# Fifteen tiles of a vector-by-matrix product: from GpSimd and ScalarE to TensorE

## The chip, the cores and the metric

The kernel runs on one core of a Trainium2 chip. A core has five engines that run side by side, each with its own queue of instructions in program order: TensorE (PE in the profile, with its weight loads shown apart as PEld), VectorE (DVE), ScalarE (ACT), GpSimd (POOL) and SyncE (SP), which issues most of the transfers from the chip's memory. The metric is the device time of one execution in microseconds (us), and the median of the runs counts.

## The reference

The program is one encoder block on 256 tokens of width 1024, in float32. What the change touches is the first line of it, the adaLN modulation: one vector of 1024 numbers goes through silu and a 1024 x 6144 matrix, and the six parts of the result shift, scale and gate everything else.

```
c_act = silu(c)
ada = c_act @ w_ada + b_ada
shift1, scale1, gate1, shift2, scale2, gate2 = split(ada, 6)

h = rms_norm(x, norm1_g) * (1 + scale1) + shift1
proj = h @ w_in
mixed = concat(rms_norm(windowed_gqa(...)), rms_norm(neighbourhood_attention(...)))
x = x + gate1 * (mixed @ w_out)
h2 = rms_norm(x, norm2_g) * (1 + scale2) + shift2
x = x + gate2 * peer(h2, w_query, sub_keys, u_experts, v_experts)
return rms_norm(x, final_g)
```

`peer` picks experts for each token out of 16,384 and costs by far the most: two matrices of 16,384 x 1024 are read whole.

## The kernel before

The execution falls into two halves. In the first, up to about 224 us, a planner orders everything from the modulation to the queries of `peer`; in the second, lines 1366 to 1583 write out by hand the passes over the two expert matrices, 128 tiles of 128 x 1024 each (lines 1507 and 1557), with rows gathered beside them by GpSimd (line 1421).

In the first half each piece of work is a job: it names one engine (or several to choose from) with a cost in us, the jobs that it needs, and the buffers or PSUM banks that it takes and frees. `run_plan` (line 295) tries 300 random orders with those costs, keeps the one in which TensorE ends first, and emits the instructions in that order. On each engine they then stand in a fixed order. So a changed cost or engine moves instructions all over the first half, and `ROUNDS`, `SEED` and the costs set the order.

All weight tiles are 128 partitions x 1024 float32 (512 KB), loaded by SyncE in the order of `STREAM` (lines 62 and 687) into nine early buffers and then eight buffers used in turn; a load waits until its buffer is free. What becomes of a tile:

- `w_in`, `w_out` and `w_query` tiles are split into a high and a low half so that a matmul of three fast products gives float32 precision: ScalarE writes the high half (line 626), VectorE or GpSimd subtracts it for the low half (line 630, later 398). The matmuls are lines 806 (the first twelve tiles, all eight chunks of the input in turn) and 442 (the rest), 24 instructions of 256 columns a tile.
- `w_ada` tiles (48, one for each 128 outputs) are laid out with the output on the partitions. `ca` holds silu(c) copied to all partitions. On VectorE one instruction multiplies the tile by `ca` and sums along the row (line 606). Fifteen tiles, those of `ON_POOL`, are done in two steps instead: GpSimd multiplies (line 598), ScalarE sums (line 601). All fifteen belong to gate1, scale2 and shift2. Eight more, of gate2, are done in the second half on VectorE.

Between the input projections and the output projection stand eight pairs of heads: scores (lines 925, 927), bias and maximum on VectorE (945), exponent on ScalarE (949), weights (982), transposes (999, 1002), values (1021, 1025), and the norms (750). Gate1 is first used at line 1077, shift2 and scale2 at 1092 to 1107. The first half ends with the sums for the second norm (line 750 again), two queries in float32 (1113), one query in split halves (1144), and from line 1358 the scores of `peer`.

Of the kernel before, what the change touches and what calls it, by code (L numbers as in the profile page):

```python
# [12 lines left out]
AF = mybir.ActivationFunctionType  # L13
# [3 lines left out]
P = 128  # L17
D = 1024
NC8 = 8
# [16 lines left out]
NCST = _o  # L36

SHIFT1, SCALE1, GATE1, SHIFT2, SCALE2, GATE2 = range(6)
ON_POOL = {(GATE1, 0), (GATE1, 2), (GATE1, 3), (GATE1, 5), (GATE1, 7), (SCALE2, 0), (SCALE2, 1), (SCALE2, 2), (SCALE2, 4), (SCALE2, 5), (SCALE2, 6), (SHIFT2, 1), (SHIFT2, 2), (SHIFT2, 3), (SHIFT2, 4)}
RAW = 4  # L40
SETTLE = 6.0
SETS = (64, 32)
# [17 lines left out]
LO_POOL = 1  # L60
# [5 lines left out]
def kernel(ctx: ExitStack, tc: tile.TileContext, xT, crow, vecs, cst, w_ada, w_in, w_out,  # L66
# [11 lines left out]
    V, S, PE, G = nc.vector, nc.scalar, nc.tensor, nc.gpsimd  # L78
# [7 lines left out]
    ada = keep.tile([P, 6, 8], F32, name="ada")  # L86
# [3 lines left out]
    cs = keep.tile([P, 8], F32, name="cs")  # L90
# [54 lines left out]
    def add(alts, *deps, take=(), free=(), lag=0.0, after=None, rows=P):  # L145
        return Job(alts, deps, take, free, lag, after, rows)
# [174 lines left out]
    MM = 0.1095  # L321
# [16 lines left out]
    tiles = {}  # L338
# [125 lines left out]
    ca = carve(D)  # L464
# [52 lines left out]
    def silu(y, x):  # L517
        S.activation(y, x, AF.Exp, scale=-1.0)
        V.tensor_scalar(y, y, 1.0, None, op0=ALU.add)
        V.reciprocal(y, y)  # L520
        V.tensor_mul(y, y, x)

    silu(c8t[:8], c8[:8])
    for w, part in ((0, SCALE1), (1, SCALE2)):
        a0 = VEC["b_ada"][0] + part * 8
        V.scalar_tensor_tensor(gb[:, w, :], vec[:, a0:a0 + 8], 1.0, v_("g2" if w else "g1"),
                               op0=ALU.add, op1=ALU.mult)
# [19 lines left out]
    cas = []  # L547
    for w in range(2):
        key = ("ca", w)
# [6 lines left out]
        m = add([("pe", 0.86, spread_c)], take=[("bank", key)], rows=8)  # L556
# [33 lines left out]
    column = {}  # L590

    def load_ada(part, c):
        key = ("ada", part, c)
        m = load(w_ada[part, c], key)
        col = ada[:, part, c:c + 1]
        if (part, c) in ON_POOL:
            def mul():
                G.tensor_mul(tiles[key], tiles[key], ca)

            def total():  # L600
                S.activation(tiles[key], tiles[key], AF.Copy, accum_out=col)

            m = add([("pool", 2.3, mul)], m, *cas)
            column[part, c] = add([("act", 1.04, total)], m, free=[key])
        else:
            column[part, c] = add([("dve", 1.15, lambda: V.scalar_tensor_tensor(
                tiles[key], tiles[key], 1.0, ca, op0=ALU.mult, op1=ALU.mult, accum_out=col))], m, *cas, free=[key])

    halved = {}
# [4 lines left out]
    def load_w(kind, i):  # L614
        key = ("w", kind, i)
        m = load(SRC[kind][i], key)
        hkey = ("h", kind, i)
        held_key[kind, i] = hkey
        if (kind, i) in WHOLE or kind == "q" and i < NQ:
            halved[kind, i] = whole[kind, i] = m  # L620
            held_key[kind, i] = key
            return

        def high():
            halves[kind, i] = new_halves(got(hkey))
            S.activation(halves[kind, i][0], tiles[key].rearrange("p (c n) -> p c n", n=P), AF.Copy)

        def low(e):
            hi, lo = halves[kind, i]
            e.tensor_sub(lo, tiles[key].rearrange("p (c n) -> p c n", n=P), hi.bitcast(F32))  # L630

        a = add([("act", 0.95, high)], m, take=[("split", hkey)])
        halved[kind, i] = add([("dve", 1.14, lambda: low(V))] + [("pool", 2.3, lambda: low(G))] * LO_POOL, a, free=[key])


    lscr = dram.tile([8, 512], F32, name="lscr")
# [1 line left out]
    def line_mm():  # L638
        PE.matmul(take_bank("line").rearrange("p a b -> p (a b)")[:8, :], t5s[:32], onehs[:32], start=True, stop=True)

    m = add([("pe", 0.86, line_mm)], take=[("bank", "line")], rows=32)
    m = add([("dve", 0.65, lambda: V.tensor_add(line[:8], tiles["line"].rearrange("p a b -> p (a b)")[:8, :], maska[:8]))],
            m, free=["line"])
# [122 lines left out]
    m = None  # L766
    for i in range(4):
        a = add([op("act", c_act(512), S.activation, sq[:, 2 * i:2 * i + 2, :], xs[:, 2 * i:2 * i + 2, :],
                    AF.Square)], xin[i])
        if i:  # L770
            a = add([op("dve", c_dve(512), V.tensor_add, sq[:, 0:2, :], sq[:, 0:2, :], sq[:, 2 * i:2 * i + 2, :])], a, m)
        m = a
# [865 lines left out]
def _layout(np, i):  # L1638
    def cols(v):
        return v.reshape(-1, P).T  # L1640

    def tiles(w):
        return w.reshape(8, P, -1, P).transpose(2, 1, 0, 3).reshape(-1, P, D)

    pa = np.array([j + 4 * s for j in range(4) for s in range(2)])
    fa = (pa[:, None] * 64 + np.arange(64)[None]).reshape(-1)
    vec = np.concatenate([
        cols(i["c"][0]),
        i["b_ada"][0].reshape(6, 8, P).transpose(2, 0, 1).reshape(P, 48),
        cols(i["norm1_g"][0]), cols(i["norm2_g"][0]), cols(i["final_g"]),  # L1650
        cols(i["out_norm_a"][0][fa]), cols(i["out_norm_b"][0]),
        np.broadcast_to(i["sink_a"][0][pa][None], (P, 8)),
    ], axis=1)
    w_in = i["w_in"][0]
    order = [np.arange(512, 640)] + [fa[j * P:(j + 1) * P] for j in range(4)] + [np.arange(640, 768)]
    for j in range(4):
        for s in range(3):
            order.append(768 + 512 * s + j * P + np.arange(P))
    w_in = tiles(w_in[:, np.concatenate(order)]).reshape(18, P, 8, P)
    first = []  # L1660
    for cp in range(4 if KT == 12 else 0):
        for c in (2 * cp, 2 * cp + 1):
            first.append(w_in[0:8, :, c].transpose(1, 0, 2))
        first.append(w_in[8:12, :, 2 * cp:2 * cp + 2].transpose(1, 2, 0, 3).reshape(P, 8, P))
    for c in range(8 if KT == 16 else 0):
        for k in range(2):
            first.append(w_in[8 * k:8 * k + 8, :, c].transpose(1, 0, 2))
    w_in = np.concatenate([np.stack(first), w_in[KT:]]).reshape(18, P, D)
    w_out = i["w_out"][0]
    w_out = np.concatenate([w_out[:512][fa], w_out[512:]], axis=0)  # L1670
    w_out = w_out.reshape(2, 4, P, 4, 2, P).transpose(0, 3, 2, 4, 1, 5).reshape(8, P, D)
    rpb = np.stack([i["rpb_b"][0].reshape(4, 2, 465)[:, :, 108 + 31 * r:264 + 31 * r] for r in range(4)])
    rpb = rpb.transpose(2, 0, 1, 3).reshape(-1)
    return {
        "xT": i["x"][0].T.reshape(8, P, T).transpose(1, 0, 2),
        "crow": i["c"].reshape(8, P),
        "vecs": vec,
        "cst": _constants(np),
        "w_ada": i["w_ada"][0].T.reshape(6, 8, P, D),
        "w_in": w_in,  # L1680
        "w_out": w_out,
        "w_query": tiles(i["w_query"][0]),
        "t5": i["t5_table"][:, pa],
        "rpb": rpb,
        "skT": i["sub_keys"][0].reshape(16, P, P).transpose(2, 0, 1),
        "uT": i["u_experts"][0].reshape(NE, P, 8, P).transpose(0, 3, 2, 1).reshape(NE, P, D),
        "uE": i["u_experts"][0],
        "vE": i["v_experts"][0],
    }
# [20 lines left out]
```

## Time and profile before

| | |
|---|---|
| median of 3 runs | 850.65 us (848.18 to 851.6) |
| the profiled execution's own time | 850.8 us |
| its span in the profile | 849.0 us |
| TensorE busy | 775.2 us, 91% |
| VectorE busy | 593.1 us, 70% |
| ScalarE busy | 268.0 us, 32% |
| GpSimd busy | 330.6 us, 39% |
| mean granted TensorE clock | 0.976 of full speed |
| bytes moved | 289.27 MB, 341 GB/s over the span |

The span is the time from the first to the last instruction that the profile shows; what lies around it, 1.8 us here, is not shown. "Busy" counts an engine's instructions whatever they wait for inside; an instruction that takes longer than its like is busy all that time. Shares over the span hide that the two halves have different limits, so the rows below are by stretch.

### The profile page before, as it was taken

How to read it: one execution, taken by the hardware profiler on the slowest of the kernel's cores; microseconds unless marked ns; L12 is line 12 of the kernel's file. 1: busy time of each engine (PE TensorE's matmuls, PEld its weight loads, DVE VectorE, ACT ScalarE, POOL GpSimd, SP SyncE). 2: the span in 40 equal slices, each digit the busy share in tenths (PEclk: the TensorE clock that was granted, in tenths of full speed). 3: DMA queues.
4: the chain of work that ended last, by engine and by line, in shares of the span. 5: the costliest groups of instructions: out<-in, count | busy, mean ns of one | idle time of the engine just before them, and what ended most of it. 6: DMA issues, size and time to landing. Idle time of an engine off the chain costs nothing.

```text
span 849.0 us, 15375 instructions
## 1 busy us (share of the span) xinstructions
PE 775.2 (91%) x5846; PEld 753.9 (89%) x5846; DVE 593.1 (70%) x1308; ACT 268.0 (32%) x741; POOL 330.6 (39%) x271
## 2 busy tenths in 40 slices
PE   3998786789799999999999999999999989899894
PEld 1997575689799999999999999999999988899893
DVE  6999999887677999569998775644435444453534
ACT  4456675456231112179876521000000000000003
POOL 2545686456314436412233233533333333332300
PEclk9999998999999999999999999999999999999997
DMA  8995666095768999999999999999999999999951
GB/s 328 408 328 206 223 227 234 0 348 202 259 229 297 392 413 395 416 413 361 359 378 374 401 371 416 415 412 416 415 416 415 414 415 416 415 413 418 414 205 50
DMA packets 81212, 289.27 MB, mean 341 GB/s; under 512 B 9281, under 2 KB 10825, under 8 KB 81010
## 3 DMA queue, kind: packets, MB, share of 16 engines
q1 hardware_dynamic: 36352, 125.60, 38.5%
q0 software_dynamic: 27776, 100.79, 30.2%
q10 hardware_dynamic: 17010, 61.89, 18.4%
q8 instruction: 46, 0.75, 0.4%
q14 instruction: 28, 0.23, 0.1%
HBM read 287.18 MB, written 1.07 MB: 340 GB/s over the span
## 4 chain that ended last, share of the span: by engine, by line
PE 34%; DMA 28%; issue 5%; DVE 3%; POOL 3%; ACT 0%; DVEq 0%; ACTq 0%; POOLq 0%
PE b L1507 27%; DMA row<-in_vE,big 24%; PE b L1557 4%; DMA raw<-in_vE,big 3%; PE b L1474 2%; DVE accg L1443 1%; POOL row L1421 1%; DMA row<-in_uT 1%; POOL raw L1421 1%; DMA row<-in_vE 1%; PE b L1342 1%; PE b L1562 0%; POOL big L1421 0%; DVE big L1443 0%; POOL lo L398 0%
## 5 line engine op out<-in xcount | busy, mean ns | idle before, releaser
L1507 PE MATMUL b<-big 128*128 128x160 f32 x928 | 134.3, 302 | 4.0 <-ACT big L1489 4.0
L1557 PE MATMUL b<-big 128*128 128x160 f32 x944 | 131.0, 299 | 5.0 <-DMA big<-in_vE 4.2
L1557 PEld LDWEIGHTS b<-big 128*128 128x128 f32 x944 | 129.0, 190 | 5.7 <-DMA big<-in_vE 4.7
L1557 PE MATMUL b<-big,row 128*128 128x160 f32 x864 | 125.5, 305 | 7.4 <-DMA row<-in_vE 7.4
L1507 PEld LDWEIGHTS b<-big 128*128 128x128 f32 x928 | 128.4, 191 | 4.2 <-ACT big L1489 4.2
L1557 PEld LDWEIGHTS b<-big,row 128*128 128x128 f32 x864 | 121.8, 194 | 8.1 <-DMA row<-in_vE 4.3
L1507 PE MATMUL b<-big,row 128*128 128x160 f32 x752 | 106.6, 300 | 0.0
L1507 PEld LDWEIGHTS b<-big,row 128*128 128x128 f32 x752 | 103.0, 190 | 0.0
L540 ACT ACTIVATE big<-xs 128x256 f32<-128x256 f32 (+1 forms) x20 | 9.1, 457 | 283.8 <-DVE xs L540 273.8
L1421 POOL DMA_INDIRECT row<-in_vE,big x48 | 49.9, 1039 | 88.0 <-DVE accg L1443 58.5
L1443 DVE SCALAR_TENSOR_TENSOR accg<-row,big,accg 128x1024 f32<-128x1024 f32 x32 | 41.2, 1286 | 51.2 <-DMA row<-in_vE,big 48.4
L442 PE MATMUL b<-hb,hi 128*128 128x256 f32 x432 | 65.5, 295 | 1.9 <-DVE hb L540 1.9
L1421 POOL DMA_INDIRECT raw<-in_vE,big x36 | 37.2, 1033 | 70.5 <-DVE accg L1443 45.5
L1421 POOL DMA_INDIRECT row<-in_uE,big x37 | 39.6, 1071 | 61.9 <-DVE big L1493 29.2
L1489 ACT ACTIVATE big<-b 128x160 f32<-128x160 f32 (+23 forms) x110 | 29.0, 266 | 104.3 <-PE b L1507 85.4
L442 PEld LDWEIGHTS b<-hb,hi 128*128 128x128 f32 x432 | 58.2, 199 | 3.9 <-DVE hb L540 2.1
L1421 POOL DMA_INDIRECT raw<-in_uE,big x34 | 34.5, 1015 | 63.6 <-DVE raw L1434 29.0
L1443 DVE SCALAR_TENSOR_TENSOR accg<-raw,big,accg 128x1024 f32<-128x1024 f32 x23 | 29.6, 1285 | 38.2 <-DMA raw<-in_vE,big 38.1
L1465 ACT ACTIVATE oh<-iota,ebf 128x128 f16<-128x128 f16 x160 | 51.0, 394 | 13.2 <-PE b L1474 9.4
L1421 POOL DMA_INDIRECT big<-in_uE,big x25 | 25.7, 1028 | 70.1 <-issue 29.3
L442 PE MATMUL b<-hb,lo 128*128 128x256 f32 x216 | 33.1, 291 | 6.6 <-DVE lo L630 5.0
L442 PEld LDWEIGHTS b<-hb,lo 128*128 128x128 f32 x216 | 28.7, 194 | 8.6 <-DVE lo L630 5.6
(212 smaller groups left out, 1381.2 us busy)
## 6 DMA issues: line engine op xcount, KB each, us to landing
big<-in_uT SPq DMA_DIRECT2D x36, 512.0 KB
big<-in_w_ada SPq DMA_DIRECT2D x33, 512.0 KB
big<-in_vE SPq DMA_DIRECT2D x31, 512.0 KB
row<-in_vE SPq DMA_DIRECT2D x29, 512.0 KB
big<-in_vE ACTq DMA_DIRECT2D x28, 512.0 KB
row<-in_vE ACTq DMA_DIRECT2D x25, 512.0 KB
row<-in_uT ACTq DMA_DIRECT2D x24, 512.0 KB
row<-in_uT SPq DMA_DIRECT2D x23, 512.0 KB
```

Source lines behind the costliest of these rows:

```text
L442: PE.matmul(ps, w[:, wc, :], r[:, rc, :], start=(n == 0), stop=(n == last))
L540: return (e, cost, lambda: f(*a, **k))
L1342: PE.matmul(px[:, c * P:(c + 1) * P], rep[:, 4 * i + c, :], ident, start=True, stop=True)
L1421: G.indirect_dma_start(row, None, uE if k < GT else vE, bass.IndirectOffsetOnAxis(ap=cidx[:, k % GT:k % GT + 1], axis=0))
L1443: V.scalar_tensor_tensor(accg[w], row, ag[:, k - GT:k - GT + 1], accg[w], op0=ALU.mult, op1=ALU.add)
L1465: S.activation(oh1[:, k, :], iota1, AF.Square, scale=-1.0, bias=ebf[:, t0 + k:t0 + k + 1])
L1474: PE.matmul(pg[:, k, :], pr[:, i, :, k], oh1[:, k, :], start=(i == 0), stop=(i == 1))
L1489: S.activation(gz[:, e, t:], ps[:, 0, t:ND], AF.Gelu_apprx_tanh)
L1507: PE.matmul(ps[:, 0, 0:ND], w[:, c, :], h2[:, c, GT:], start=(c == 0), stop=(c == NC8 - 1))
L1557: PE.matmul(acc[c][:, 0, GT:], w[:, c, :], gz[:, e, :], start=(e == 0), stop=(e == NE - 1), skip_group_check=True)
```

## The change

Each of the fifteen tiles is transposed block by block on the host, so that its eight blocks of 128 x 128 can be stationary operands. `cs`, an 8-column tile, gets silu(c) as a column for each block. A tile's product is then eight float32 matmuls of one column into a PSUM bank, and ScalarE copies that column out. Two planning costs change too: 1.15 to 1.3 for the VectorE form of a `w_ada` tile and 1.14 to 1.22 for a low half on VectorE.

```
@@ the set, by another name
-ON_POOL = {(GATE1, 0), (GATE1, 2), (GATE1, 3), (GATE1, 5), (GATE1, 7), (SCALE2, 0), (SCALE2, 1), ...
+ON_PE = {(GATE1, 0), (GATE1, 2), (GATE1, 3), (GATE1, 5), (GATE1, 7), (SCALE2, 0), (SCALE2, 1), ...
@@ before the first plan
     silu(c8t[:8], c8[:8])
+    silu(cs, v_("c"))
@@ load_ada
-        if (part, c) in ON_POOL:
-            def mul():
-                G.tensor_mul(tiles[key], tiles[key], ca)
-
-            def total():
-                S.activation(tiles[key], tiles[key], AF.Copy, accum_out=col)
-
-            m = add([("pool", 2.3, mul)], m, *cas)
-            column[part, c] = add([("act", 1.04, total)], m, free=[key])
+        if (part, c) in ON_PE:
+            def products_c():
+                w = tiles[key].rearrange("p (c n) -> p c n", n=P)
+                pc = take_bank(("adac", part, c))
+                for k in range(NC8):
+                    PE.matmul(pc[:, 0, 0:1], w[:, k, :], cs[:, k:k + 1], start=(k == 0), stop=(k == NC8 - 1))
+
+            m = add([("pe", 16 * MM, products_c)], m, take=[("bank", ("adac", part, c))], free=[key])
+            column[part, c] = add([("act", 0.25, lambda: S.activation(
+                col, tiles["adac", part, c][:, 0, 0:1], AF.Copy))], m, free=[("adac", part, c)])
         else:
-            column[part, c] = add([("dve", 1.15, lambda: V.scalar_tensor_tensor(
+            column[part, c] = add([("dve", 1.3, lambda: V.scalar_tensor_tensor(
@@ load_w
-        halved[kind, i] = add([("dve", 1.14, lambda: low(V))] + [("pool", 2.3, lambda: low(G))] * LO_POOL, a, free=[key])
+        halved[kind, i] = add([("dve", 1.22, lambda: low(V))] + [("pool", 2.3, lambda: low(G))] * LO_POOL, a, free=[key])
```

The changed file has lines of its own numbers: its 602 is the new matmul, and 598 to 1149 of the kernel before stand two lines later in it (925 is 927, 999 is 1001).

GpSimd, from the bias of the second kind of heads on. Before, multiplications of `w_ada` tiles (line 598) stand through the whole row:

```order
L660 TENSOR_TENSOR big<-big 128x4x128 x3
L598 TENSOR_TENSOR big<-big 128x1024 x2
L598 TENSOR_TENSOR raw_667<-raw_667,big 128x1024
L598 TENSOR_TENSOR raw_724<-raw_724,big 128x1024
L598 TENSOR_TENSOR big<-big 128x1024
L982 TENSOR_TENSOR big<-big 128x2x256 x2
L598 TENSOR_TENSOR raw_884<-raw_884,big 128x1024
L598 TENSOR_TENSOR big<-big 128x1024 x3
```

Now three low halves (632 there, 630 before) stand ahead of the bias, and one behind it:

```order
L632 TENSOR_TENSOR lo_229<-raw_180,hi_228 128x1024
L632 TENSOR_TENSOR lo_360<-big,hi_359 128x1024
L632 TENSOR_TENSOR lo_431<-big,hi_430 128x1024
L541 TENSOR_TENSOR hb<-big,hb 128x256
L662 TENSOR_TENSOR big<-big 128x4x128 x3
L984 TENSOR_TENSOR big<-big 128x2x256
L632 TENSOR_TENSOR lo_1011<-big,hi_1010 128x1024
L541 TENSOR_TENSOR hb<-big,hb 128x256
```

All fifteen long multiplications are gone from it; four low halves are left, as before, of which three have moved ahead.

TensorE, behind the first scores of the heads. Before, score and projection matmuls alternate (`hb` holds the split input, `hi` and `lo` a tile's halves, `b` a PSUM bank):

```order
L925 MATMUL b_675<-big 128x256
L925 MATMUL b_676<-big 128x256
L442 MATMUL b_689<-hb,hi_616 128x256 x8
L442 MATMUL b_689<-hb,lo_617 128x256 x8
L442 MATMUL b_689<-hb,hi_616 128x256 x8
L862 MATMUL b_732<-big 128x128 x2
```

Now tiles of the modulation stand there, eight calls each; a call is two instructions:

```order
L602 MATMUL b_676<-cs,big 128x1 x8
L602 MATMUL b_694<-cs,big 128x1 x8
L602 MATMUL b_716<-cs,raw_670 128x1 x8
L927 MATMUL b_734<-big 128x256
L927 MATMUL b_735<-big 128x256
L927 MATMUL b_734<-big 128x256
L927 MATMUL b_735<-big 128x256
L602 MATMUL b_746<-cs,raw_713 128x1 x8
L1001 MATMUL b_762<-big 128x128 x4
L442 MATMUL b_771<-hb,hi_672 128x256 x8
L442 MATMUL b_771<-hb,lo_673 128x256 x8
```

Four tiles of one-column matmuls with four score calls and four transposes between them stand in a row there; further on four tiles stand in a row with nothing between.

TensorE, ahead of the last four tiles of the output projection. Before, the last values of the heads and two sums:

```order
L442 MATMUL b_1287<-hb,hi_1254 128x256 x4
L1025 MATMUL b_1326<-big 64x16x4 x8
L1025 MATMUL b_1339<-big 64x16x4 x8
L1025 MATMUL b_1349<-big 64x16x4 x8
L750 MATMUL b_1372<-big 128x256 x2
L442 MATMUL b_1381<-hb,hi_1272 128x256 x4
```

Now the last three modulation tiles stand among them:

```order
L1027 MATMUL b_1437<-big 64x16x4 x8
L1027 MATMUL b_1451<-big 64x16x4 x8
L602 MATMUL b_1463<-cs,big 128x1 x8
L1004 MATMUL b_1483<-big 128x128 x4
L602 MATMUL b_1490<-cs,big 128x1 x8
L752 MATMUL b_1500<-big 128x256
L1027 MATMUL b_1503<-big 64x16x4 x8
L602 MATMUL b_1512<-cs,raw_1086 128x1 x8
L752 MATMUL b_1500<-big 128x256
L442 MATMUL b_1527<-hb,hi_1318 128x256 x4
```

Of the fifteen tiles all stand between the first scores of the heads and the last four tiles of the output projection.

## Rows read from the trace of the kernel before

**Rows 1.** The page: what the transfers moved in each 21.2 us slice.

```profile
GB/s 328 408 328 206 223 227 234 0 348 202 259 229 297 392 413 395 416 413 361 359 378 374 401 371 416 415 412 416 415 416 415 414 415 416 415 413 418 414 205 50
```

**Rows 2.** By stretch: length, busy us of PE, PEld, DVE, ACT, POOL; clock, DMA.

```profile
21.20:61.20 40.00, 38.76 (x290) 38.12 (x290) 38.73 (x55) 20.72 (x33) 20.21 (x14) 1.00 0.99 375
61.20:155.80 94.60, 73.65 (x600) 63.85 (x600) 93.51 (x175) 59.09 (x151) 64.78 (x32) 0.93 0.59 206
155.80:177.40 21.60, 15.28 (x66) 12.66 (x65) 18.73 (x46) 11.95 (x30) 7.92 (x8) 0.84 0.26 92
177.40:224.60 47.20, 45.62 (x373) 44.20 (x372) 37.42 (x176) 25.02 (x48) 30.96 (x14) 1.00 0.68 256
224.60:849.00 624.40, 595.10 (x4508) 591.02 (x4506) 390.85 (x833) 142.65 (x468) 200.67 (x194) 0.98 0.95 374
```

**Rows 3.** Groups by line, 61.2 to 155.8 us: busy us, mean ns, idle before.

```profile
L598 POOL TENSOR_TENSOR big<-big 128x1024 f32<-128x1024 f32 x11 | 32.0, 2933 | 4.9 <-DMA big<-in_w_ada 4.9
L606 DVE SCALAR_TENSOR_TENSOR raw<-raw,big 128x1024 f32<-128x1024 f32 x6 | 14.6, 2435 | 0.0
L630 DVE TENSOR_TENSOR lo<-raw,hi 128x1024 fp32r<-128x1024 f32 x7 | 13.3, 1903 | 0.0
```

**Rows 4.** Lines 630 and 962: ns minimum/median/maximum, when, forms.

```profile
L630 DVE TENSOR_TENSOR lo<-big,hi x13: 1214/1221/2590, 15.0 to 147.1; 128x1024 fp32r<-128x1024 f32 x13
...
L962 DVE TENSOR_TENSOR big<-big,vec x8: 147/152/2310, 68.5 to 97.6; 128x2 f32<-128x2 f32 x8
```

**Rows 5.** What TensorE waited for, 61.2 to 155.8 us: total, times, longest.

```profile
PE b L442 <- DVE lo L630: 5.0, 3, 2.2
```

**Rows 6.** TensorE in order of time: start, us, work, idle before.

```profile
73.75 1.38 PE L442 MATMUL b<-hb,lo 128*128 128x256 f32 x8 [2.21 <-DVE lo L630]
74.92 3.55 PE L442 MATMUL b<-hb,hi 128*128 128x256 f32 x16
78.31 1.12 PE L442 MATMUL b<-hb,lo 128*128 128x256 f32 x8
...
86.34 1.12 PE L442 MATMUL b<-hb,lo 128*128 128x256 f32 x8
87.30 1.12 PE L442 MATMUL b<-hb,hi 128*128 128x256 f32 x8
```

**Rows 7.** TensorE's weight loads in order of time, at the end.

```profile
828.48 0.33 PEld L1562 LDWEIGHTS b<-big,accg 128*128 128x128 f32 x2
...
828.72 0.30 PEld L1562 LDWEIGHTS b<-big 128*128 128x128 f32 x2
828.95 0.57 PEld L1557 LDWEIGHTS b<-big,row 128*128 128x128 f32 x4
```

**Rows 8.** TensorE in order of time, the start of the execution.

```profile
4.78 3.75 PE L554 MATMUL b<-big 8*128 8x128 f32 x16 [4.78 <-DMA big<-in_cst]
8.46 1.87 PE L639 MATMUL b<-big 32*8 32x512 f32 x2
...
26.06 3.79 PE L806 MATMUL b<-hb,hi 128*128 128x256 f32 x16 [1.09 <-POOL hb L540]
...
30.89 2.08 PE L806 MATMUL b<-hb,hi 128*128 128x256 f32 x16
```

**Rows 9.** The chain that ended last: start, us, what; 128-column float32 matmuls.

```profile
243.98 1.78 PE b L1342 x16
```

**Rows 10.** All engines, end of the output projection and the sums behind it.

```profile
155.72 0.64 PE L442 MATMUL b<-hb,hi 128*128 128x256 f32 x4
159.07 2.58 DVE L540 TENSOR_TENSOR big<-big 128x256 f32<-128x256 f32 x1
163.96 2.08 PE L750 MATMUL b<-big 128*128 128x256 f32 x4 [3.50 <-DVE big L540]
```

**Rows 11.** Line 1123, and VectorE at the start.

```profile
L1123 ACT ACTIVATE big<-b x2: 149/151/153, 172.2 to 173.0; 128x1 f32<-128x1 f32 x2
...
7.36 0.69 DVE L540 TENSOR_TENSOR big<-big 128x512 f32<-128x512 f32 x1 [3.11 <-ACT big L540]
```

More of the change, by code (lines that the diff above doesn't have):

```diff
@@ L38 @@
 SHIFT1, SCALE1, GATE1, SHIFT2, SCALE2, GATE2 = range(6)
-ON_POOL = {(GATE1, 0), (GATE1, 2), (GATE1, 3), (GATE1, 5), (GATE1, 7), (SCALE2, 0), (SCALE2, 1), (SCALE2, 2), (SCALE2, 4), (SCALE2, 5), (SCALE2, 6), (SHIFT2, 1), (SHIFT2, 2), (SHIFT2, 3), (SHIFT2, 4)}
+ON_PE = {(GATE1, 0), (GATE1, 2), (GATE1, 3), (GATE1, 5), (GATE1, 7), (SCALE2, 0), (SCALE2, 1), (SCALE2, 2), (SCALE2, 4), (SCALE2, 5), (SCALE2, 6), (SHIFT2, 1), (SHIFT2, 2), (SHIFT2, 3), (SHIFT2, 4)}
 RAW = 4
@@ L1673, in _layout @@
     rpb = rpb.transpose(2, 0, 1, 3).reshape(-1)
+    ada = i["w_ada"][0].T.reshape(6, 8, P, D).copy()
+    for part, c in ON_PE:
+        ada[part, c] = ada[part, c].T.reshape(8, P, P).transpose(1, 0, 2).reshape(P, D)
     return {
@@ L1678, in _layout @@
         "cst": _constants(np),
-        "w_ada": i["w_ada"][0].T.reshape(6, 8, P, D),
+        "w_ada": ada,
         "w_in": w_in,
```

## The prediction

> **What bounds the kernel now.** I read the transfers by slice first, then the busy time by stretch, then the groups and waits of the stretch in which the fifteen tiles stand, then TensorE and its waits in order of time.
>
> The fifteen tiles are worked on between 61.2 and 155.8 us. From 177.4 us on nothing of the change is left, so the first question is whether time won before it reaches the end. In the eighth slice the transfers moved 0 GB/s [rows 1], and from 155.8 to 177.4 us only 92 GB/s, a DMA share of 0.26 [rows 2]: every buffer is full and the next loads wait for the first half to let go of them. From 224.6 us TensorE is busy 595 of 624 us at a DMA share of 0.95 [rows 2]. That second half starts with what the buffers hold, the same amount each time, so I carry a shift at 177.4 us to the end one to one.
>
> From 61.2 to 155.8 us VectorE is busy 93.5 of 94.6 us, TensorE 73.7, GpSimd 64.8, ScalarE 59.1 [rows 2]. Much of VectorE's time is waiting inside instructions. A low half takes 1.22 us at the median and 2.59 at worst; an addition of two numbers a partition takes 0.15 and at worst 2.31 [rows 4], about the length of a multiplication on GpSimd, 2.93 us [rows 3]. So VectorE is held up while GpSimd works, and TensorE waits for VectorE: 5.0 us for low halves alone [rows 5].
>
> **The change part by part.** Sums are against the profiled execution, 850.8 us (span 849.0 and 1.8 around it); the median, 850.65, is the same within what can be told apart, and I put the differences on the median. About 0.5%, 4.25 us, is what a measurement of this kernel can tell from no change.
>
> *The column silu(c).* One instruction on ScalarE and three on VectorE, on 8 columns, before 7.36 us, where VectorE sits idle 3.1 us for the squares of x [rows 11]. Cost 0; without that cover under 1 us.
>
> *0 to 61.2 us.* The new order gives VectorE three low halves less and GpSimd three more, and VectorE some short subtractions of GpSimd's. TensorE is busy 38.8 of 40 us, VectorE 38.7 [rows 2]: both are full, and neither loses or gains more than a few short instructions. I take 0, within 2 us either way.
>
> *GpSimd and ScalarE, 61.2 to 155.8 us.* Fifteen multiplications of 2.93 us [rows 3], 44 us, leave GpSimd; the fifteen sums leave ScalarE, and fifteen copies of one column at 0.15 us [rows 11] come to it. Neither engine sets the end here (64.8 and 59.1 of 94.6 us), so what counts is what VectorE gets back. Six modulation tiles average 2.44 us and seven low halves 1.90 [rows 3] where 1.22 is the undisturbed length: 7.3 and 4.8 us of waiting in these two groups, which is at least 12 us of VectorE's 93.5. With one long GpSimd instruction left behind the bias, VectorE needs about 81 of the 95 us and is no longer what ends last.
>
> *TensorE, 61.2 to 155.8 us.* It was idle 94.6 - 73.65 = 20.95 us. At a granted clock of 0.93 [rows 2] another 0.07 x 94.6 = 6.6 us of its busy time was lost pulses, so its work is 67.0 us at full clock. The change adds 15 tiles x 8 calls x 2 instructions = 240, each with a weight load of 128 x 128 float32. The trace has no one-column matmul; the nearest are the 64- and 32-column sums at the end, whose loads follow each other at 0.24 us (828.48 to 828.72) and 0.23 us (to 828.95) for two [rows 7], 0.1175 us each. 240 x 0.1175 = 28.2 us. 67.0 + 28.2 = 95.2 us: TensorE is now full from end to end. The idle time was behind VectorE, which now has slack; of 20.95 us I leave 1 (bounds 0 and 6). The stretch takes 96.2 us, +1.6.
>
> The Trainium skill ("TensorE: Matmul & The Clock Gate", Part 2, LDWEIGHTS) puts a load of 128 columns at 107 ns, which I work out from its formula as an estimate. By that the addition would be 25.6 us and the forecast 2.6 us lower; the 64- and 32-column rows at 117.5 ns decide here.
>
> *155.8 to 177.4 us.* The second norm's sum starts at 163.96 us, 7.6 us after the output projection's last instruction ended (155.72 + 0.64), and waited for VectorE 3.5 us; VectorE had stood 2.58 us in one addition beside a low half on GpSimd [rows 10]. In the new order no low half is on GpSimd there and VectorE has no backlog. The steps that must follow the last tile (gate, add, square, add, of 256 columns) are an estimated 3.5 us from instructions of 0.35 us for 256 columns (half of 0.69 for 512 [rows 11]) with a hand-over each: -4.1. The sum itself took 2.08 us for four instructions [rows 10] where 128 columns take 0.111 us at full clock [rows 9] and 256 thus 0.22: -0.9 or so, if the shorter gap keeps the clock. Together -5.0 (bounds -6 and 0).
>
> *The clock.* So far the sum is +1.6 - 5.0 = -3.4, if TensorE's clock holds. TensorE's clock has two levels, 1.2 and 2.4 GHz. After the wait that ended at 73.75 us, 2.2 us long, sixteen instructions took 74.92 to 78.31, 3.39 us, at half clock, where full clock gives 0.96 us for eight (86.34 to 87.30), 1.92 for sixteen [rows 6]: 1.47 us lost. Being busy is not enough. From 4.78 to 10.3 us TensorE worked without a gap, but with 8 and 32 of the 128 rows, and sixteen 128-column instructions took 3.7 us, 0.23 each, twice the 0.111 of full clock [rows 8, 9]; with all 128 rows it was still at half at 26.06 (sixteen in 3.79) and at full by 30.89 (sixteen in 2.08) [rows 8]. A stretch of weight loads with one column each fills TensorE's time and streams next to nothing; no row shows what the clock does then. The order has three long ones: four tiles with four score calls and four transposes among them (7.5 us of loads, the rest an estimated 1.5), four tiles alone (7.5), and three with values, transposes and sums (5.6, the rest an estimated 3.0). The cost is bounded below by 0, the clock holding. Treated like the wait of rows 6, each of the three costs the dense tiles behind it 1.47 us, 4.4 in all, and the 4.5 us of other small work inside take twice as long: 8.9 us. If the loads slow with the clock as well, up to 20.6 us more. Of these I take 8.9: it is priced by the nearest rows, and nothing shows a load at half clock.
>
> Sum: -3.4 + 8.9 = +5.5, 856 us. TensorE takes the place of VectorE, and pays for light work in clock.
>
> **The rivals.**
> *The clock holds.* Then the sum is -3.4: 847.3 us, not slower. Place: the three runs of one-column matmuls; price against the forecast: the 8.9 us; it decides once less than 3.4 us of them occur. For it: there is no idle gap. Against it: rows 8. The Trainium skill (same page, Part 1, "What's actually happening") lets the gate follow how busy the engine has been, which read plainly is this rival; rows 8 show a busy stretch at half clock.
>
> *The relief goes further.* The clock holds, no wait is left in the middle stretch (-1) and the first gains 2: -6.4, 844 us. For it: nearly all TensorE waits were behind VectorE. Against it: TensorE is full, so VectorE's slack has nothing left to shorten.
>
> *The loads don't overlap.* Two loads take 0.33 us with 0.12 between their starts [rows 7], so one alone takes about 0.21. If one-column matmuls hide nothing of it, 240 x (0.21 - 0.1175) = 22 us come on top of the clock-holding case: 869 us. It makes the kernel slower by over 0.5% from 0.149 us a load on, (3.4 + 4.25)/240 above 0.1175. Against it: with 32 columns the loads still followed at 0.1175.
>
> *It doesn't reach the end.* If the second half's start were set by the transfers and not by the buffers, 850.65 stays. Against it: the idle transfers [rows 1, 2].
>
> **How the numbers follow.** Forecast (clock falls) 0.50: its own range 851.7 (dense tiles alone suffer, 4.4) to 866 (half of the 20.6 comes on top), 0.36 of it slower and 0.14 within 0.5%. Clock holds 0.30: 847.3 is just inside the bound at 846.4, so 0.16 faster and 0.14 the same. Further relief 0.10, faster. Unhidden loads 0.07, slower. No shift 0.03, the same. Faster 0.26, same 0.31, slower 0.43. The range takes in the forecast's and both clock-holding cases but for their ends: 842 to 866.
>
> **What would show it.** Right: the granted clock of the middle stretch under 0.93 although TensorE waits little; dense tiles behind runs of one-column matmuls at about 0.21 us an instruction; VectorE's low halves near 1.22 us, and idle time on it; the second norm's sum about 4 us behind the last tile. Wrong: full clock behind those runs, so that the output projection ends before 157 us; loads in them far from 0.1175 us; TensorE waiting long for a tile's transfer or a PSUM bank, which I counted inside the 1 us; or a second half that is not simply moved.

## The result, and the profile after

The changed kernel takes 861.7 us in the median of four runs (858.51 to 862.8), the kernel before 850.72: a ratio of 1.0132 [1.0113, 1.0151], 11.0 us slower. In a second comparison it took 860.3 us (858.92 to 862.19) against 850.3, 1.0122 [1.0100, 1.0143]. The profile is that of the 858.51 us execution, the fastest of the four (span 856.7 us). The forecast of 856 us has the direction right and half of the size. In the code after, the new matmuls and their copies are at lines 602 and 605; line 540 of before is 541, 606 is 608, 630 is 632, 750 is 752, 806 is 808.

By stretch, cut at about the same work as in [rows 2] (start:end, length, busy us of PE, PEld, DVE, ACT, POOL, granted clock, DMA share, GB/s):

```profile
21.20:65.70 44.50, 38.67 (x282) 38.13 (x280) 41.93 (x57) 17.95 (x28) 24.22 (x12) 0.92 0.93 349
65.70:172.20 106.50, 106.50 (x845) 99.79 (x844) 71.03 (x182) 55.61 (x157) 14.52 (x13) 0.86 0.57 193
172.20:186.90 14.70, 11.76 (x62) 9.73 (x60) 12.30 (x26) 7.81 (x21) 7.27 (x9) 1.00 0.11 39
186.90:234.00 47.10, 45.57 (x369) 44.15 (x370) 38.13 (x182) 25.34 (x48) 30.95 (x14) 1.00 0.70 252
234.00:856.70 622.70, 594.64 (x4509) 590.98 (x4508) 390.96 (x833) 142.88 (x468) 203.00 (x194) 0.98 0.95 376
```

Four things are to be seen; the times are those of the instructions themselves. The first stretch ends 4.6 us later (scores from 65.79 us, before 61.18). From the first scores to the last output tile it takes 106.5 us, before 95.2 (61.18 to 156.36), with TensorE busy in all of it at a granted clock of 0.86. From there to the second half it takes 14.6, before 21.0. The rest takes 669.8 us, before 671.6. +4.6 + 11.3 - 6.4 - 1.8 = +7.7 us of span. That is the fastest execution; the 3.3 us that the median has more lie in executions that left no trace. In the second profile of the same kernel the four are +4.7, +9.8, -6.4 and +1.1, together +9.2.

The first stretch. VectorE in order of time, and below it GpSimd (start, us, work, idle before and what ended it):

```profile
29.53 2.32 DVE L541 TENSOR_TENSOR ada<-ada,vec 128x1 f32<-128x1 f32 x1
...
40.41 2.56 DVE L541 TENSOR_TENSOR hb<-big,hb 128x256 fp32r<-128x256 f32 x1
...
46.93 3.42 DVE L608 SCALAR_TENSOR_TENSOR big<-big 128x1024 f32<-128x1024 f32 x1
...
54.68 1.21 DVE L541 TENSOR_TENSOR ada<-ada,vec 128x1 f32<-128x1 f32 x1
55.81 1.40 DVE L541 SCALAR_TENSOR_TENSOR mod<-ada,vec,gb 128x1 f32<-128x1 f32 x1
```

```profile
28.63 3.20 POOL L632 TENSOR_TENSOR lo<-raw,hi 128x1024 fp32r<-128x1024 f32 x1 [0.45 <-ACT hi L628]
39.27 3.43 POOL L632 TENSOR_TENSOR lo<-big,hi 128x1024 fp32r<-128x1024 f32 x1 [7.43 <-DVE mod L541]
46.44 2.83 POOL L632 TENSOR_TENSOR lo<-big,hi 128x1024 fp32r<-128x1024 f32 x1 [3.74 <-ACT hi L628]
...
53.51 6.11 POOL L662 TENSOR_TENSOR big<-big 128x512 f32<-128x512 f32 x3
```

The first three of VectorE's take 0.15, 0.42 and 1.22 us elsewhere. Each ends 0.02, 0.27 or 1.08 us behind the low half on GpSimd beside it (29.53 + 2.32 = 31.85, and 28.63 + 3.20 = 31.83), which is a little less than its own length, so VectorE loses 2.2, 2.1 and 2.2 us. The Trainium skill ("SBUF — State Buffer", Terms) says of the pair of ports that VectorE and GpSimd share that the loser "fully blocks" for the whole instruction; these rows agree.

Those 6.5 us stand against the 3.7 us of work that VectorE was spared, 2.8 us in net. The delay then grew: the last two of the rows, which prepare the last normalized block and take 0.15 and 0.21 us elsewhere, now stood beside the bias on GpSimd (line 662) and lost another 2.2 us. With the low halves on VectorE, in a run below, they are at 51.93 and 52.01 us and over before the bias begins at 53.40.

What came of it on TensorE:

```profile
54.20 1.12 PE L808 MATMUL b<-hb,hi 128*128 128x256 f32 x8
58.35 1.22 PE L808 MATMUL b<-hb,hi 128*128 128x256 f32 x8 [3.03 <-ACT hb L541]
59.41 1.87 PE L808 MATMUL b<-hb,lo 128*128 128x256 f32 x8
61.07 2.87 PE L808 MATMUL b<-hb,hi 128*128 128x256 f32 x16
...
65.79 0.49 PE L927 MATMUL b<-big 64*128 64x256 f32 x2
```

The last normalized block comes late and TensorE stands idle 3.03 us. Eight instructions behind the gap take 1.87 us where 1.12 is usual, and the sixteen after them 2.87 us where 2.08 is (granted clock 0.51 from 59.41 to 61.07 us, and 0.67 to 63.78). Before had no such gap there.

The middle stretch, TensorE in order of time (answers to [rows 6]):

```profile
75.93 3.55 PE L602 MATMUL b<-cs,raw 128*128 128x1 f32 x16
79.41 2.08 PE L927 MATMUL b<-big 64*128 64x256 f32 x8
81.41 3.57 PE L602 MATMUL b<-cs,raw 128*128 128x1 f32 x16
84.85 1.09 PE L1001 MATMUL b<-big 128*128 128x128 f32 x4
85.59 2.06 PE L442 MATMUL b<-hb,hi 128*128 128x256 f32 x8
87.45 1.91 PE L442 MATMUL b<-hb,lo 128*128 128x256 f32 x8
89.15 1.57 PE L442 MATMUL b<-hb,hi 128*128 128x256 f32 x8
90.56 0.38 PE L864 MATMUL b<-big 128*128 128x128 f32 x2
90.78 1.84 PE L602 MATMUL b<-cs,big 128*128 128x1 f32 x16
92.49 0.72 PE L442 MATMUL b<-hb,hi 128*128 128x256 f32 x4
```

There is no gap, and still half clock: the granted clock is 0.50 from 75.93 to 79.41 us and 1.00 from 90.78 to 92.49. One tile's sixteen loads take 90.78 to 92.49, 1.71 us, 0.107 each, at full clock, and 75.93 to 79.41, 3.48 us, 0.218 each, at half: the loads slow with the clock. The Trainium skill ("TensorE: Matmul & The Clock Gate", Part 2, LDWEIGHTS) gives a load as columns divided by 1.2, in ns, an estimated 107 ns for 128 columns; the full-clock row agrees with it, the half-clock row is twice that.

The transfers by slice (GB/s) have no empty slice any more, as [rows 1] had one; the eighth and ninth are the low ones:

```profile
GB/s 328 408 302 222 230 236 175 94 126 311 176 292 250 366 414 388 416 415 387 349 370 375 388 383 409 415 414 415 414 415 416 415 415 415 414 414 416 415 257 50
```

TensorE's waits for low halves [rows 5] are gone, and VectorE is relieved as forecast and more: 71.0 us busy. The low halves and the small additions of [rows 4] now read as below; the second group of low halves had a median of 1559 ns and a maximum of 3386 before.

```profile
L632 DVE TENSOR_TENSOR lo<-big,hi x12: 1201/1219/1758, 14.3 to 168.3; 128x1024 fp32r<-128x1024 f32 x12
L632 DVE TENSOR_TENSOR lo<-raw,hi x12: 1207/1216/1226, 34.1 to 171.9; 128x1024 fp32r<-128x1024 f32 x12
...
L964 DVE TENSOR_TENSOR big<-big,vec x8: 152/154/161, 71.5 to 120.5; 128x2 f32<-128x2 f32 x8
```

The end of the stretch, as in [rows 10], reads on TensorE

```profile
171.68 0.64 PE L442 MATMUL b<-hb,hi 128*128 128x256 f32 x4
...
175.59 1.13 PE L752 MATMUL b<-big 128*128 128x256 f32 x4 [0.66 <-DVE big L541]
...
186.93 1.16 PE L1360 MATMUL b<-big 128*128 128x128 f32 x8 [0.17 <-ACT big L541]
```

The second norm's sum starts 3.3 us behind the last output tile (7.6 before) and takes 1.13 us where it took 2.08.

### The profile page after: what moved, and what is told of

It is laid out like the page before. It is cut to its first block, busy times and chain, and to the rows that moved or that the text cites. A ratio compares the mean times of both kernels' runs of the same rounds, so it can differ in the third digit from the quotient of the medians.

```text
span 856.7 us, 15823 instructions
## 1 busy us (share of the span) xinstructions
PE 805.7 (94%) x6086; PEld 788.7 (92%) x6086; DVE 569.4 (66%) x1310; ACT 259.4 (30%) x735; POOL 285.8 (33%) x252
## 4 chain that ended last, share of the span: by engine, by line
PE 37%; DMA 25%; issue 5%; POOL 3%; DVE 2%; ACT 0%; DVEq 0%; ACTq 0%; POOLq 0%
PE b L1509 27%; DMA row<-in_vE,big 22%; PE b L1559 7%; PE b L1476 2%; DMA raw<-in_vE,big 2%; DMA row<-in_uT 1%; POOL row L1423 1%; POOL raw L1423 1%; DMA big<-in_vE 1%; DVE accg L1445 1%; PE b L1344 0%; PE b L1564 0%; POOL big L1423 0%; POOL lo L398 0%; DVE big L541 0%
## 5 line engine op out<-in xcount | busy, mean ns | idle before, releaser
L1559 PE MATMUL b<-big 128*128 128x160 f32 x944 | 134.8, 304 | 9.5 <-DMA big<-in_vE 8.7
L1559 PEld LDWEIGHTS b<-big 128*128 128x128 f32 x944 | 132.4, 194 | 10.5 <-DMA big<-in_vE 9.5
L1509 PE MATMUL b<-big 128*128 128x160 f32 x928 | 134.9, 302 | 4.8 <-ACT big L1491 4.8
L1509 PEld LDWEIGHTS b<-big 128*128 128x128 f32 x928 | 129.0, 192 | 5.0 <-ACT big L1491 5.0
L1559 PE MATMUL b<-big,row 128*128 128x160 f32 x864 | 121.6, 300 | 1.0 <-DMA row<-in_vE 1.0
L1559 PEld LDWEIGHTS b<-big,row 128*128 128x128 f32 x864 | 118.4, 190 | 1.3 <-DMA row<-in_vE 1.3
L1509 PE MATMUL b<-big,row 128*128 128x160 f32 x752 | 106.6, 300 | 0.0
L1509 PEld LDWEIGHTS b<-big,row 128*128 128x128 f32 x752 | 103.0, 190 | 0.0
L1423 POOL DMA_INDIRECT row<-in_vE,big x48 | 51.9, 1081 | 81.9 <-DVE accg L1445 52.9
L1445 DVE SCALAR_TENSOR_TENSOR accg<-row,big,accg 128x1024 f32<-128x1024 f32 x32 | 41.1, 1284 | 46.0 <-DMA row<-in_vE,big 45.9
L442 PE MATMUL b<-hb,hi 128*128 128x256 f32 x432 | 65.6, 296 | 0.0
L442 PEld LDWEIGHTS b<-hb,hi 128*128 128x128 f32 x432 | 58.5, 200 | 0.6 <-issue 0.3
L808 PE MATMUL b<-hb,hi 128*128 128x256 f32 x192 | 29.0, 307 | 12.5 <-ACT hb L541 12.5
L808 PEld LDWEIGHTS b<-hb,hi 128*128 128x128 f32 x192 | 27.4, 216 | 13.7 <-ACT hb L541 13.7
```

The costliest lines, as they stand in the source:

```text
L442: PE.matmul(ps, w[:, wc, :], r[:, rc, :], start=(n == 0), stop=(n == last))
L808: PE.matmul(tiles["acc", n // 2][:, n % 2, :], w[:, b, :], r[:, c, :], start=(c == 0 and t == 0 and n % 2 == 0), stop=(c == NC8 - 1 and t ...
L1423: G.indirect_dma_start(row, None, uE if k < GT else vE, bass.IndirectOffsetOnAxis(ap=cidx[:, k % GT:k % GT + 1], axis=0))
L1445: V.scalar_tensor_tensor(accg[w], row, ag[:, k - GT:k - GT + 1], accg[w], op0=ALU.mult, op1=ALU.add)
L1509: PE.matmul(ps[:, 0, 0:ND], w[:, c, :], h2[:, c, GT:], start=(c == 0), stop=(c == NC8 - 1))
L1559: PE.matmul(acc[c][:, 0, GT:], w[:, c, :], gz[:, e, :], start=(e == 0), stop=(e == NE - 1), skip_group_check=True)
```

## The experiments

My theory: of the 11 us, 5 come from the low halves that the new order gives to GpSimd ahead of the scores, and the others from a clock that one-column matmuls don't hold and at which the loads themselves take twice as long; with both mended the change is a gain. The rivals are that TensorE is simply overfull, whatever its clock, or that the new order as such is worse. All kernels but the last keep the changed kernel's order, so only what stands at a place differs. Medians of before on the same chips were 850.05 to 850.48 us.

**128 columns behind each load**

```diff
-PE.matmul(pc[:, 0, 0:1], w[:, k, :], cs[:, k:k + 1], ...)
+PE.matmul(pc[:, 0, 0:P], w[:, k, :], ones, ...)
```

> The changed kernel in its own order, with 128 columns (of the constant ones, so the fifteen tiles are not multiplied by silu(c)) behind each of the 240 weight loads instead of one. Theory: the runs of one-column matmuls let the clock fall and the loads themselves then take 0.215 us instead of 0.107; with 128 columns the clock holds, each instruction takes 0.111 us, and of the 14.9 us lost to the clock between 65.7 and 172.2 us some 11 come back: 851 us. Rival: the loads fill TensorE whatever the clock does, and the half clock has another cause (the small score and transpose work around them): the clock of that stretch stays near 0.86 and the time at 861 to 863 us.

847.8 us (846.33 to 848.73), 0.9967 [0.9953, 0.998]. The middle stretch, and the work that stood at half clock above:

```profile
65.70:158.30 92.60, 92.60 (x844) 86.50 (x844) 71.58 (x182) 55.72 (x157) 14.52 (x13) 1.00 0.64 224
```

```profile
74.53 1.95 PE L602 MATMUL b<-big,raw 128*128 128x128 f32 x16
76.41 1.13 PE L927 MATMUL b<-big 64*128 64x256 f32 x8
77.47 2.05 PE L602 MATMUL b<-big,raw 128*128 128x128 f32 x16
79.36 0.60 PE L1001 MATMUL b<-big 128*128 128x128 f32 x4
79.72 1.20 PE L442 MATMUL b<-hb,hi 128*128 128x256 f32 x8
```

The same 844 matmuls and loads, 128 times the columns in 240 of them, and 13.9 us less, at a clock of 1.00. Length times granted clock is what a stretch would take at full clock: 106.5 x 0.86 = 91.6 us, about the 92.6 measured here. TensorE is full in both, so the rival that it is overfull whatever its clock falls.

**Low halves on VectorE**, with one column

```diff
-[("pool", 2.3, lambda: low(G))]
+[("pool", 2.3, lambda: low(V))]
```

> The changed kernel in its own order; the four low halves that the new order gives to GpSimd (at 28.6, 39.3, 46.4 and 113.3 us) are computed by VectorE at the same places. Theory: each of the first three held VectorE for 2.1 to 2.3 us in an instruction beside it, which made the output of the last normalized block late and left TensorE idle 3.0 us and then at half clock; VectorE has to do 3 x 1.22 us more but is held 6.5 us less, so the first stretch is about 4 us shorter: 857.5 us. Rival: VectorE is simply full in that stretch, and 3.7 us more of work makes it later: 864 to 865 us.

The edit moves all four low halves of GpSimd, the fourth at 113 us. The time is 859.9 us, but 852.52 in the profiled execution and 858.41 to 860.68 in the others; 1.0125 [1.0096, 1.0154]. In the profile the gap is gone (53.95 to 60.76 without a wait), and the scores start 5.0 us earlier:

```profile
56.83 2.08 PE L808 MATMUL b<-hb,hi 128*128 128x256 f32 x16
58.75 1.12 PE L808 MATMUL b<-hb,lo 128*128 128x256 f32 x8
59.71 1.12 PE L808 MATMUL b<-hb,hi 128*128 128x256 f32 x8
60.76 1.13 PE L927 MATMUL b<-big 64*128 64x256 f32 x8
```

So VectorE wasn't too full for 3.7 us more, and the mechanism holds; but the end moved by 5 us or more in one execution of five only.

**Both**

> The changed kernel in its own order with both edits: the four low halves of GpSimd on VectorE, and 128 columns of ones (not silu(c)) behind each load. Theory: the 5 us that the low halves on GpSimd cost ahead of the first scores are real, and in the typical execution with one-column matmuls they are given back by the clock alone; with the clock held they reach the end: 847.8 - 5 = 843 us. Rival: what is won before the scores is lost again later whatever the clock does (buffers, transfers): 847 to 848 us.

843.21 us (842.16 to 844.16), 0.9928 [0.9907, 0.9950]: with the clock held, 4.6 of the 5 us reach the end (847.8 - 843.2; 4.2 if each is taken against the median of before on its own chip). The middle takes 92.6 us with the fourth low half on either engine, so the gain is that of the first three. The rival, that it is lost later anyway, falls.

**The same once more, and the changed kernel beside it**

> The changed kernel with the four low halves on VectorE once more (the run before had 852.5 us in the profiled execution and 858 to 861 us in the others, at a lower mean clock). Theory: one-column matmuls hold the clock in some executions and not in others, so the times spread over more than 5 us and the granted clock tells them apart; this profile again shows full TensorE and the clock as the only difference. Rival: the spread comes from the transfers or the second half, with the same clock ahead of 170 us in every execution.

> The changed kernel itself once more, beside the one with the low halves on VectorE on the same chip. Theory: 858 to 863 us, a little above the other; half clock stands where runs of one-column matmuls and the small work among them are, but not at the same places as in the first profile. Rival: the clock falls at the same places for the same times in every execution.

859.74 us (857.75 to 861.32) and 860.3 us. These four executions spread over 3.6 us, all nine over 8.8. This time the kernel with the low halves on VectorE had its profile at 861.32 us. The first row is the middle stretch of its 852.52 us execution, the second that of this one:

```profile
60.80:164.10 103.30, 103.30 (x844) 96.84 (x844) 71.10 (x183) 55.56 (x157) 12.18 (x12) 0.88 0.60 202
```

```profile
62.00:171.60 109.60, 109.60 (x844) 102.65 (x844) 71.29 (x184) 55.75 (x157) 12.03 (x12) 0.83 0.57 192
```

One kernel, the same 844 instructions: 103.3 x 0.88 = 90.9 and 109.6 x 0.83 = 91.0 us at full clock. So 6.3 us between two executions are the clock alone. From the second half on they take 672.0 and 672.3 us, so the rival that looks for the spread there falls. The changed kernel's second profile has 105.0 us at 0.87.

Where the clock is lost was expected to change from one profile to the next, and that was a miss. Both profiles of the changed kernel have half clock at the same three places, in and behind the three runs of tiles that the prediction names: at a granted clock of 0.50 stand 76 to 88, 104 to 108 and 156 to 160 us of the first profile, and 76 to 84, 100 to 108 and 156 to 160 us of the second. Only the lengths differ. In the 852.52 us execution the third run kept full clock, as its last tile shows (below it the same tile in the changed kernel; 3.58 us too in the execution of 861.32 us):

```profile
150.15 1.95 PE L602 MATMUL b<-cs,raw 128*128 128x1 f32 x16
```

```profile
155.26 3.58 PE L602 MATMUL b<-cs,raw 128*128 128x1 f32 x16
```

So the two costs don't simply add. With one-column matmuls eight of nine executions of the kernel with the low halves on VectorE show little of its earlier start at the end. In the one of them that was traced, a lower clock in the middle took it back (109.6 us against 105.0); the others are known only by their mean clock over the span, 0.958 to 0.966, where the execution of 852.52 us had 0.973. Why the clock is lower behind the earlier start stays open; no run tells it.

**One of eight products**

```diff
-for k in range(NC8):
-    PE.matmul(pc[:, 0, 0:1], w[:, k, :], cs[:, k:k + 1], ...)
+PE.matmul(pc[:, 0, 0:1], w[:, 0, :], cs[:, 0:1], start=True, stop=True)
```

> The changed kernel in its own order, with one of the eight products of each of the fifteen tiles (seven of eight are left out): 30 loads instead of 240. Theory: TensorE is what ends last between 65.7 and 172.2 us, and 210 loads cost it 22.5 us at full clock and up to 45 at half; without them it waits for VectorE again (71 us busy of 106), so not all comes back: 835 to 842 us. Rival: the new order around the tiles is what costs, then most of the 11 us stay and the time is 855 us or more.

838.08 us (837.23 to 839.05), 0.9867 [0.9837, 0.9896]. The middle takes 87.9 us, TensorE busy 77.7. Without seven eighths of the products the new order is 12 us faster than before, so the order of the other work is not what makes the changed kernel slow.

**The order with GpSimd's multiplications**

```diff
-PE.matmul(pc[:, 0, 0:1], ...)   # eight
+G.tensor_mul(tiles[key], tiles[key], ca)
...
-S.activation(col, tiles["adac", part, c][:, 0, 0:1], AF.Copy)
+S.activation(tiles[key], tiles[key], AF.Copy, accum_out=col)
```

> The order of the changed kernel with the operations of the kernel before: at the place of the eight matmuls of a tile GpSimd multiplies it, at the place of the copy ScalarE sums it; all the rest stands as in the changed kernel, with silu(c) still computed. Theory: the new order costs about 4.5 us before the first scores by itself, and behind that GpSimd's multiplications hold VectorE as before: 855 to 860 us. Rival: the order costs nothing, only the matmuls do: 849 to 852 us.

860.95 us, 1.0146 [1.0111, 1.0182]. This says little of the order, because ScalarE's sums now wait for GpSimd and hold up what is queued behind them, and one of them even for the next load of the buffer:

```profile
ACT big L602 <- POOL big L599: 12.7, 5, 4.8
...
ACT big L602 <- DMA big<-in_w_ada: 1.4, 1, 1.4
```

The next run leaves the sums out:

> The order of the changed kernel once more with the multiplications of the fifteen tiles on GpSimd at the place of the matmuls; the fifteen sums on ScalarE are left out (a column of other data is copied in their place), because there the next load of a buffer had come in ahead of the sum. Theory: with GpSimd's multiplications in this order VectorE is held as in the kernel before, while the order was laid out without them: 855 to 861 us, near the changed kernel's time, for another reason. Rival: the order is no worse for GpSimd's multiplications than the old one: 850 us or less.

857.67 us (855.46 to 857.9), 1.0086 [1.0061, 1.0111]. TensorE waits for VectorE again. The longest wait is for the sum ahead of the output projection's last tiles, at 152.20 us (4.1 us before, at 141.53); the wait of [rows 10] is 0.65 us here.

```profile
PE b L749 <- DVE big L541: 7.0, 1, 7.0
PE b L1020 <- DVE big L1006: 5.2, 2, 3.8
```

The old operation in the new order is as slow as the changed kernel, with VectorE busy 94.3 of 103.0 us instead of TensorE 106.5 of 106.5. The order was laid out for other operations, so this run says little on what it costs under the matmuls; the run with one of eight products says more.

**All fifteen on VectorE**

```diff
-PE.matmul(pc[:, 0, 0:1], ...)   # eight, and the copy on ScalarE
+V.scalar_tensor_tensor(tiles[key], tiles[key], 1.0, ca, op0=ALU.mult, op1=ALU.mult, accum_out=col)
```

> The changed kernel in its own order, without the 240 matmuls: VectorE multiplies and sums the fifteen tiles where the matmuls stood, as it does with the other modulation tiles, and also makes the four low halves of GpSimd. Theory: GpSimd's multiplications of before cost VectorE about as much in waiting as they took off it. VectorE's 71 us between the first scores and the last output tile become 71 + 15 x 1.3 = 90.5 with nothing that holds it, TensorE is no longer full, and the stretch is about as long as before (94.6 us); with the first stretch 5 us and the sums of the second norm 6 us shorter: 842 to 848 us. Rival: VectorE's instructions stand where TensorE's were planned, so both wait for each other: 855 us or more.

844.01 us (842.48 to 845.01), 0.9930 [0.9906, 0.9955]. VectorE is busy 87.1 of 93.5 us there, with fifteen tiles and a low half more than it has there in the changed kernel; before, with the fifteen multiplications on GpSimd, it was busy 93.5 of 94.6 us [rows 2]. So those multiplications had saved VectorE nothing. The 6 us to before are not their price alone, since the order and the low halves differ too.

**silu(c) read 128 times**, and the low halves on VectorE

```diff
-PE.matmul(pc[:, 0, 0:1], w[:, k, :], cs[:, k:k + 1], ...)
+PE.matmul(pc[:, 0, 0:P], w[:, k, :], cs[:, k:k + 1].to_broadcast([P, P]), ...)
```

> As the run with both edits, but the 128 columns are the column of silu(c) read 128 times, so that nothing is left out. Theory: TensorE streams a repeated column like any other and the time is that of the run with ones: 843 us. Rival: a column read 128 times doesn't hold the clock, or streams slower than 0.111 us an instruction: 850 us or more.

843.1 us (842.6 to 844.63), 0.9928 [0.9905, 0.9951], and the middle is that of the run with ones to the tenth:

```profile
60.70:153.30 92.60, 92.60 (x844) 86.50 (x844) 70.96 (x183) 55.71 (x157) 12.11 (x12) 1.00 0.65 225
```

**Half of the tiles, in the old order and in a new one**

```diff
+ON_VECTOR = {(GATE1, 2), (GATE1, 5), (SCALE2, 0), (SCALE2, 2), (SCALE2, 6), (SHIFT2, 1), (SHIFT2, 3)}
...
+if (part, c) in ON_VECTOR:
+    V.scalar_tensor_tensor(tiles[key], tiles[key], 1.0, ca, ...)
```

> The changed kernel in its own order, with seven of the fifteen tiles (every second one) on VectorE where their matmuls stood, eight on TensorE with the column of silu(c) read 128 times, and the four low halves of GpSimd on VectorE. Theory: with all fifteen on TensorE it has no idle time left between the first scores and the last output tile, with all on VectorE that one is full; 7 x 16 loads at 0.11 us are 12.3 us off TensorE, and 7 x 1.3 = 9.1 us go to VectorE, which was busy about 16 of 20 us there. Most of the 12.3 us come back: 832 to 836 us. Rival: TensorE then waits for VectorE as it does with all fifteen there: 840 to 844 us.

839.98 us (835.94 to 841.61), 0.9872 [0.9838, 0.9906]: a miss by 4 us, at the edge of the rival's 840 to 844. The middle takes 87.3 us, 5.3 less and not 12; TensorE is busy 82.3 of them and waits 2.1 us for transfers of tiles and 2.9 us for VectorE and ScalarE.

```diff
-ON_PE = {...}   # fifteen
+ON_PE = {(GATE1, 0), (GATE1, 3), (GATE1, 7), (SCALE2, 1), (SCALE2, 4), (SCALE2, 5), (SHIFT2, 2), (SHIFT2, 4)}
-LO_POOL = 1
+LO_POOL = 0
```

> The same eight tiles on TensorE with the column read 128 times, the other seven on VectorE and no low half on GpSimd, and now the order laid out anew for that (the planner is told that low halves run on VectorE alone and that seven more tiles are VectorE's). Theory: as the run in the old order or a little better: 828 to 836 us. Rival: a new order loses elsewhere as much as it wins here: 840 us or more.

831.08 us (827.74 to 832.52), 0.9780 [0.9760, 0.9801], the fastest, with nothing left out. First stretch and middle:

```profile
21.20:59.90 38.70, 36.77 (x289) 36.36 (x287) 37.88 (x56) 17.36 (x25) 17.37 (x12) 1.00 1.03 392
59.90:140.50 80.60, 80.60 (x731) 73.93 (x730) 73.08 (x181) 57.66 (x162) 23.81 (x22) 1.00 0.67 241
```

731 instructions without a gap at full clock: 12.0 us less than with fifteen tiles, the 12.3 that the loads are worth.

## Why the prediction was wrong

By its own terms, 0 + 1.6 - 5.0 + 8.9 = +5.5 us, against +11.0. Measured by removal, each kernel against the median of before on its own chip, the change with both mends is worth -6.8 us (843.2 - 850.05), the low halves on GpSimd +4.2 and the clock +13.7; that makes the +11.0. Taken off in the other order, while the clock falls, the low halves are worth 0.6 us (860.3 - 859.7 on one chip), which the spread covers. Two steps failed, the first stretch at 0 and the loads at half clock at 0; a third, TensorE's work in the middle, was put too high and hid part of them.

- *silu(c) at 0*: nothing waits for it; TensorE's first dense run starts at 19.37 us, before at 21.19.
- *0 to 61.2 us at 0 within 2*: this step failed, +4.6 us. The prediction took "VectorE three low halves less and GpSimd three more" as a fair exchange. It had just said that VectorE is held up while GpSimd works [rows 4], and didn't apply it to the three that move: 3.7 us off VectorE, 6.5 us of holding on it, and 2.2 us more when the delayed instructions ran into the bias, right ahead of a block that TensorE waits for.
- *TensorE, 61.2 to 155.8 us at +1.6*: with the clock held -2.6 (92.6 against 95.2 us). It is full as forecast. Of the 4.2 us between, 1.0 is the idle time that the forecast left, 1.0 the fifteen tiles (27.2 us with 128 columns, 0.113 for each of 240, where 28.2 was reckoned), and the rest, about 2, other work that took less than the 67.0 us reckoned for full clock.
- *The tail at -5.0*: -6.4, in the run with the clock held -5.8. Right; the second norm's sum came 3.3 us behind the last tile, forecast 3.5.
- *The clock at +8.9*: right in mechanism, and the term that missed most: 13.9 us. Summing TensorE from start to start in the changed kernel and in the one with 128 columns, 4.5 us are the dense tiles of line 442 (45.9 against 41.4; forecast 4.4), 2.0 the other small work (forecast 4.5), and 7.5 the fifteen tiles' own matmuls (34.6 against 27.2). This last part was put at 0 with the words that "nothing shows a load at half clock", though its bound of 20.6 us stood beside it. With no row near, a value between 0 and 20.6 was due; with the 7.5 that came the sum would have been +13.0. One of the prediction's own signs of being wrong is this: loads far from 0.1175 us, here 0.218 at half clock.
- *One to one from there*: right within 2 us, 669.8 and 672.7 us in the two profiles against 671.6.

Of the rivals, *the clock holds* (847.3) has the number of the run with 128 columns, 847.8, but by other terms: there the first stretch is +4.5, the middle -2.6, the end of the first half -5.8 and the rest +1.9. *The loads don't overlap* is out: 0.107 us each. *It doesn't reach the end* is out, since the rest moved with the shift within 2 us. *The relief goes further* (844) has the number of the run with both mends, but the changed kernel isn't that run, and the first stretch there gains 0.5 us and not 2.

## What to carry to other kernels

Price a stream of matmuls with few columns by what it does to the clock of everything in it, its own weight loads first; a column read 128 times (a zero stride) costs no more instructions and kept the full clock here. When an order is laid out anew, look at what else moved: three subtractions that went to GpSimd cost 4 to 5 us where the clock held. And before work goes to one engine as a whole, see whether dividing it between two isn't worth more than either: eight tiles and seven took 831 us with the order laid out for them (840 in the old order), where all fifteen took 843 on TensorE and 844 on VectorE.

## What the runs showed of the hardware

- Weight loads of 128 x 128 float32 with one column each: 0.107 us at full clock, 0.218 at half.
- TensorE busy without a gap for 106.5 us had a granted clock of 0.86 with one column behind 240 loads, and 1.00 with 128. The Trainium skill ("TensorE: Matmul & The Clock Gate", Part 1, "What's actually happening") lets the gate follow how busy the engine has been; read plainly, these two rows speak against it.
- A moving column read 128 times streams like 128 columns that lie side by side: 92.6 us for the stretch in both kernels.
- The granted clock of one kernel with such work differs between executions: 0.88 and 0.83 over the same 844 instructions, 6.3 us.
- A 128 x 1 addition of VectorE took 2.32 us beside a GpSimd subtraction of 3.20 us that ended with it; elsewhere 0.15.
